# A state space mixer with its matrix products in four column groups of TensorE, and its gate placed behind two tiles of the output projection

## The chip, the cores and the metric

The kernel runs on one core of a Trainium2 chip. TensorE (PE) multiplies and writes to PSUM, VectorE (DVE), ScalarE (ACT) and GpSimd (POOL) compute, SyncE (SP) issues the DMAs. The metric is the time of one execution on the device in microseconds (us), median of the runs; lower is better.

## The reference, cut to what matters

Four network blocks work on 512 tokens of width 1024. The change touches the third, whose mixer joins a diagonal state space (256 channels in 16 groups of 16, with 64 states each) and a gated spatial unit (768 channels):

```python
def s5_mixer(u, ...):
    bb_re = z_re * br - z_im * bi
    bb_im = z_re * bi + z_im * br
    x_re = jnp.einsum('bsgh,gph->bsgp', uf, bb_re)
    x_im = jnp.einsum('bsgh,gph->bsgp', uf, bb_im)
    ...
    _, _, h_re, h_im = lax.associative_scan(combine, (a_re, a_im, x_re, x_im), axis=1)
    y = (jnp.einsum('bsgp,ghp->bsgh', h_re, c_re)
         - jnp.einsum('bsgp,ghp->bsgh', h_im, c_im))
    y = (y + d_skip.reshape(SSM_GROUPS, SSM_GROUP) * uf).reshape(bsz, s, SSM_WIDTH)
    y = jax.nn.gelu(y)
    y = y * jax.nn.sigmoid(y @ w_glu + b_glu)
...
        mix = jnp.concatenate([a_out, b_out], axis=-1) @ ev_w_out[e]
    h = h + mix
    h = h + conv_ffn(rmsnorm(h, ffn_norm_g[layer]), ...)
```

## The kernel before

All activations lie transposed, 128 channels by 512 tokens in a tile. A product of accuracy close to float32 is made of three matmuls of split operands (`mm3`, L533, whose lines L535, L536 and L537 appear in the trace): each operand is cut by `split` (L496: a cast on ACT, a subtraction on DVE) or, for weights, by `wsplit` (L510: cast L518, subtraction L519 on DVE or POOL) into a high and a low part. One `mm3` piece, as the text calls it, is one such matmul. Products of whole float32 operands show as two records each.

The order of instructions on each engine is set when the program is built: a list scheduler with a model of the engines goes through the code in priority order and fixes one order per engine. On the chip each engine then takes its instructions strictly in that order, and waits where an operand isn't there.

The stage is `ev` (L1233). It makes the 256 state space inputs `u32` (L1267, after the norms of `ev_norms`, L1212), the value half of the gated unit (192 pieces of 384 columns, in two halves), then for six heads the gate half (144 pieces of 512 columns) and `spatial` (L1294). Between them the generator `s5` (L1468) is stepped by `next(s5)`. It treats the 1024 states as eight indices `i` of 128 states; per index:

- `prepare` (L1479) forms the input matrix from B and z (ACT L1486, DVE L1487), transposes it on PE (L1491) and splits it (L1494, L1495); `inputs` (L1497) puts 32 channels three times into a tile `us` (L1502 to L1504); two matmuls (L1533) follow.
- The rotation by the tables `cs` and `sn`: four products on DVE out of PSUM (L1538, L1539, L1541, L1542), a sum and a difference on POOL (L1540, L1543).
- Two scans on DVE (L1547, L1548), and the rotation back: two products on DVE (L1550, L1552), two on POOL (L1551, L1553), one difference each on DVE (L1554, `hr`) and POOL (L1555, `hi`).
- Two float32 matmuls of 128 rows (L1522, L1523) add the result to the tile `py`, four indices to each.

When a half of 128 channels is complete: L1526, a gelu (L1527), a split. After all eight indices come the matmuls of `w_glu`, the sigmoid and the gate (L1331, L1332). The output projection takes 18 pieces per tile `f` from the gated unit (`ew_oa`) and 6 from the state space (`ew_ob`, in `rest`, L1343), 204 pieces with the 12 of `w_glu`; `resid` (L594) adds each tile to `x` and prepares the next stage (`ffn`). `scaled` (L1341) multiplies the eight tiles of `x` by the norm before they are added to.

## Time and profile before

| | |
|---|---|
| median of 3 runs | 1980.95 us (1980.42 to 1981.53) |
| the profiled execution | 1977.64 us, its span 1975.6 us, granted clock 0.984 |
| busy in the span | PE 96%, weight loads 81%, DVE 64%, ACT 47%, POOL 30% |
| the chain that ended last | PE 46%, DVE 4%, ACT 1%, issue 1% of the span in pieces that it lists by name |

The busy share of PE is that of the whole span; for the stage of the change it stands in the rows below. Of every group of instructions the rows give the number, the time that it was busy and the mean duration of one; instructions of one engine overlap by a little, so the step from one start to the next is shorter than the duration.

### The profile page before, as it was taken

The page shows a single profiled execution, that of the slowest core. Times are in us where ns is not written, and L with a number is a line of the kernel's source. Part 1 is how long each engine was busy: PE and PEld are TensorE (multiplying, and loading weights), DVE is VectorE, ACT ScalarE, POOL GpSimd, SP SyncE. Part 2 cuts the span into 40 slices and gives each one's busy share as a digit, 9 for nine tenths or more (in the row PEclk, how much of TensorE's full clock was granted, in tenths as well). Part 3 has the DMA queues.
Part 4 walks back from the last instruction along what each step waited for, and adds up shares of the span by engine and source line. Part 5 has one row for each costly group of instructions (what it writes and reads, how often), then busy time and mean ns, then how long its engine had stood idle before and what let it go on. Part 6 is the DMA issues. An engine that isn't in the chain of part 4 may idle for free.

```text
span 1975.6 us, 25804 instructions
## 1 busy us (share of the span) xinstructions
PE 1887.0 (96%) x10098; PEld 1599.0 (81%) x10098; DVE 1272.2 (64%) x1801; ACT 932.0 (47%) x1601; POOL 591.6 (30%) x514
## 2 busy tenths in 40 slices
PE   7999999999989999897889999999999999999997
PEld 4788889898879899786668888888788888888886
DVE  4422777777565555889976666666744566666666
ACT  4534677677365544756535333333422343333333
POOL 0012766654012221656630313131400002121213
PEclk8999999999999999999999999999999999999998
DMA  8531000103321111132113232223222222222221
GB/s 332 192 123 59 28 17 12 44 23 109 106 77 62 43 43 49 65 107 91 48 56 126 86 107 85 107 86 107 85 86 91 101 88 104 91 102 89 103 88 62
DMA packets 31833, 171.81 MB, mean 87 GB/s; under 512 B 3328, under 2 KB 6656, under 8 KB 14688
## 3 DMA queue, kind: packets, MB, share of 16 engines
q1 hardware_dynamic: 31712, 170.17, 24.1%
q8 instruction: 79, 1.29, 0.3%
q14 instruction: 42, 0.34, 0.1%
HBM read 168.06 MB, written 2.10 MB: 86 GB/s over the span
## 4 chain that ended last, share of the span: by engine, by line
PE 46%; DVE 4%; issue 1%; ACT 1%; POOL 0%; DVEq 0%; POOLq 0%; ACTq 0%
PE b L535 15%; PE b L537 15%; PE b L536 15%; DVE cv L1564 0%; DVE x L1683 0%; DVE hl L502 0%; DVE wl L519 0%; DVE hr L1554 0%; DVE x L598 0%; ACT wh L518 0%; PE b L624 0%; DVE yl L498 0%; DVE gt L1301 0%; POOL cv L1595 0%; DVE b L1547 0%
## 5 line engine op out<-in xcount | busy, mean ns | idle before, releaser
L535 PE MATMUL b<-hh,wh 128*128 128x512 f32 (+1 forms) x1248 | 482.2, 389 | 4.0 <-DVE uu L1305 2.7
L518 ACT CAST wh<-raw 128x1024 fp32r<-128x1024 f32 (+1 forms) x257 | 263.4, 1026 | 463.5 <-PE b L536 418.7
L536 PE MATMUL b<-hl,wh 128*128 128x512 f32 (+1 forms) x1248 | 477.6, 383 | 3.7 <-DVE hl L502 3.7
L537 PE MATMUL b<-hh,wl 128*128 128x512 f32 (+1 forms) x1248 | 477.6, 383 | 0.0
L519 DVE TENSOR_TENSOR wl<-raw,wh 128x1024 fp32r<-128x1024 f32 (+1 forms) x189 | 239.9, 1272 | 86.1 <-ACT wh L518 76.7
L519 POOL TENSOR_TENSOR wl<-raw,wh 128x1024 fp32r<-128x1024 f32 (+1 forms) x68 | 166.2, 2446 | 418.6 <-ACT wh L518 418.4
L535 PEld LDWEIGHTS b<-hh,wh 128*128 128x128 f32 x1248 | 235.3, 189 | 56.7 <-issue 7.7
L536 PEld LDWEIGHTS b<-hl,wh 128*128 128x128 f32 x1248 | 235.9, 189 | 53.6 <-DVE hl L502 4.9
L537 PEld LDWEIGHTS b<-hh,wl 128*128 128x128 f32 x1248 | 235.6, 189 | 49.5 <-issue 0.4
L1564 DVE SCALAR_TENSOR_TENSOR cv<-u,vec,cv 128x511 f32<-128x511 f32 x192 | 184.1, 959 | 41.3 <-ACT cv L1562 39.3
L1590 DVE TENSOR_TENSOR u<-b,Rp 128x512 f32<-128x512 f32 x88 | 60.8, 691 | 157.9 <-PE b L537 157.6
L535 PE MATMUL b<-ah,wh 128*128 128x512 f32 (+1 forms) x368 | 140.1, 382 | 0.0
L537 PE MATMUL b<-ah,wl 128*128 128x512 f32 (+1 forms) x368 | 140.0, 381 | 0.0
L536 PE MATMUL b<-al,wh 128*128 128x512 f32 (+1 forms) x368 | 139.8, 380 | 0.0
L1595 POOL TENSOR_TENSOR cv<-cv 128x512 f32<-128x512 f32 x44 | 57.1, 1297 | 269.3 <-DVE cv L1564 212.9
L1615 DVE TENSOR_TENSOR x<-x,b 128x512 f32<-128x512 f32 x160 | 105.7, 680 | 12.4 <-PE b L537 12.1
L535 PE MATMUL b<-wh,hh 128*128 128x256 f32 (+1 forms) x320 | 96.2, 303 | 2.6 <-ACT wh L518 2.6
L1562 ACT ACTIVATE cv<-u,vec 128x512 f32<-128x512 f32 x96 | 78.2, 814 | 35.7 <-DVE u L1590 35.7
L536 PE MATMUL b<-wl,hh 128*128 128x256 f32 (+1 forms) x320 | 93.7, 294 | 0.0
L537 PE MATMUL b<-wh,hl 128*128 128x256 f32 (+1 forms) x320 | 93.0, 292 | 0.0
L1050 DVE TENSOR_REDUCE st<-b 128x1 f32<-128x768 f32 (+1 forms) x96 | 74.1, 773 | 28.4 <-PE b L537 27.8
L1055 POOL TENSOR_SCALAR p<-p,st 128x768 f32<-128x768 f32 (+1 forms) x96 | 73.2, 764 | 56.1 <-DVE st L1054 49.5
(406 smaller groups left out, 3878.6 us busy)
## 6 DMA issues: line engine op xcount, KB each, us to landing
raw<-in_fw_up SPq DMA_DIRECT2D x44, 1024.0 KB, 4.8
raw<-in_fw_dn SPq DMA_DIRECT2D x22, 1024.0 KB, 4.8
raw<-in_ow_in SPq DMA_DIRECT2D x12, 1024.0 KB, 4.8
ada<-in_ada SPq DMA_DIRECT2D x8, 1024.0 KB, 11.4
raw<-in_mw_in SPq DMA_DIRECT2D x7, 1024.0 KB, 7.9
spare<-in_ada SPq DMA_DIRECT2D x5, 1024.0 KB, 6.5
cq<-in_ada SPq DMA_DIRECT2D x4, 1024.0 KB, 5.0
raw<-in_mw_out SPq DMA_DIRECT2D x4, 1024.0 KB, 4.9
```

The lines of the kernel that those rows point to most:

```text
L518: self.S.copy(hi, raw[:, o:o + w])
L519: (leng or self.V).tensor_tensor(lo, raw[:, o:o + w], hi.bitcast(F32), op=ALU.subtract)
L535: m(out, w[0], x[0], start=start, stop=False)
L536: m(out, w[0], x[1], start=False, stop=False)
L537: m(out, w[1], x[0], start=False, stop=stop)
L1050: V.tensor_reduce(st[:, 0:1], sv, axis=AX.XY, op=ALU.max, negate=True)
L1055: G.tensor_scalar(p[:, :nk * P], p[:, :nk * P], st[:, 2:3], 0.0, op0=ALU.mult, op1=ALU.add)
L1562: self.S.activation(v, u, AF.Identity, bias=col(3), scale=col(2))
L1564: self.V.scalar_tensor_tensor(v[:, sh:], u[:, :T - sh], col(tap), v[:, sh:], op0=ALU.mult, op1=ALU.add)
L1590: V.tensor_tensor(u, ps, R, op=ALU.mult)
L1595: G.tensor_tensor(cv[0], cv[0], cv[1], op=ALU.mult)
L1615: V.tensor_tensor(self.x[:, 4 * j + f], self.x[:, 4 * j + f], ps, op=ALU.add)
```

## The change

What it does, in six parts:

1. The input matrices are plain B, laid out by the host in the order that the matmul needs (`in_s5b`, four loads of two indices each); the factor z is put into C instead (`cz`, six small DVE operations once, and a `sel` of 128x32 that adds four groups). The transposes and `bb` go; a split of B remains once for two indices.
2. `us` gets two buffers and is copied on ACT from the split halves `uh`, `ul` (three copies of 32 rows); the subtraction on DVE goes.
3. `turned` keeps the first rotation as it was, with one scratch tile `t` for both subtrahends; it runs one index ahead of `states`.
4. `states` makes the four products of the back rotation on DVE and adds nothing; `outputs` multiplies each of the four by its 128x32 matrix into its own 32 rows of one PSUM tile (four column groups), ACT copies the tile to `po`, and a matmul with `sel` adds the four groups into 32 rows of `py`. 24 of the 40 POOL operations of the eight indices go.
5. The generator is stepped after other tiles of the value and gate parts, and `uu` and `sg` have one buffer in place of two.
6. The pieces of `ew_oa` for the first two tiles (`first(0)`, `first(1)`) stand ahead of `w_glu`; `scaled` stands behind the last product of the state space (`behind`, an order without a wait).

The diff; the lines that it takes out of `s5` are those of the listing above.

```diff
...
+    b, c = np.zeros((32, 8, 2, P), w.dtype), np.zeros((P, 8, 2, 32), w.dtype)
+    for part, nm in enumerate(("re", "im")):
+        for i in range(8):
+            for j in range(2):
+                ch, st = slice(16 * j, 16 * j + 16), slice(64 * j, 64 * j + 64)
+                b[ch, i, part, st] = f[f"s5_b_{nm}_2"][0][2 * i + j].T
+                c[st, i, part, ch] = f[f"s5_c_{nm}_2"][0][2 * i + j].T
+    a["s5b"] = np.concatenate([b.reshape(32, 4, 4 * P).transpose(1, 0, 2)] * 3, 1)
+    a["s5c"] = c.reshape(P, 8 * 2 * 32)
...
             uh, ul = yh[:, 0:2], yl
+            next(s5)
             us = []
...
-            next(s5)
...
-                    next(s5, None)
+                    if kg % 2 == half:
+                        next(s5, None)
...
-                uu = M.tile([P, T], F32, tag="uu", name="uu", bufs=2)
+                uu = M.tile([P, T], F32, tag="uu", name="uu", bufs=1)
...
+            win = self.wstream(ins["ew_oa"], 8, 2, P)
+            parts = {}
+            def first(f):
+                if f < KT:
+                    w, ps = next(win), self.b1()
+                    for k in range(6):
+                        self.mm3(ps, (w[0][:, k], w[1][:, k]), (yh[:, 2 + k], yl[2 + k]), k == 0, False)
+                    parts[f] = ps
+            first(0)
+            first(1)
             w, = self.wload(ins["w_glu"], 512)
...
-            win = self.wstream(ins["ew_oa"], 8, 2, P)
 
             def scaled(f):
                 if f < KT:
-                    V.scalar_tensor_tensor(x[:, f], x[:, f], self.vcol("final_g", f), R, op0=ALU.mult, op1=ALU.mult)
-
-            def rest(f, ps):
+                    i = V.scalar_tensor_tensor(x[:, f], x[:, f], self.vcol("final_g", f), R, op0=ALU.mult, op1=ALU.mult)
+                    self.behind(i, self.s5_last)
+
+            def rest(f):
+                scaled(f)
+                ps = parts.pop(f)
                 for k in range(2):
                     c = slice(f % 4 * P, (f % 4 + 1) * P)
                     self.mm3(ps, (wb[0][:, k, c], wb[1][:, k, c]), (yh[:, k], yl[k]), False, k == 1)
                 self.resid(f, ps, self.vcol("ffn_norm_g_2", f))
 
-            scaled(0)
-            before = None
-            for f in range(KT):
-                w = next(win)
-                scaled(f + 1)
-                ps = self.b1()
-                for k in range(6):
-                    self.mm3(ps, (w[0][:, k], w[1][:, k]), (yh[:, 2 + k], yl[2 + k]), k == 0, False)
-                if f:
-                    if f % 4 == 1:
-                        wb = self.view(self.wload(ins["ew_ob"][f // 4], 1024)[0], 512)
-                    rest(f - 1, before)
-                before = ps
+            for g in range(2):
+                first(4 * g + 2)
+                if g:
+                    rest(2)
+                first(4 * g + 3)
+                if g:
+                    rest(3)
+                wb = self.view(self.wload(ins["ew_ob"][g], 1024)[0], 512)
+                rest(4 * g)
+                first(4 * g + 4)
+                rest(4 * g + 1)
+                first(4 * g + 5)
+            rest(6)
             self.look_ahead(True, "fw_up0", 2 * NFF)
-            rest(KT - 1, before)
+            rest(7)
...
+        US = {}
+        BH, RAW = {}, {}
+        def load(n):
+            if n < 4:
+                RAW[n] = Z.tile([96, 2, 2, P], F32, tag="braw", name="braw", bufs=1)
+                self.dma(RAW[n].rearrange("p i a s -> p (i a s)"), self.ins["s5b"][n])
+        def prepare(n):
+            if n < 4:
+                BH[n] = Z.tile([96, 2, 2, P], F32R, tag="bh", name="bh", bufs=2)
+                S.copy(BH[n], RAW[n])
+                V.tensor_tensor(BH[n][64:96], RAW[n][64:96], BH[n][64:96].bitcast(F32), op=ALU.subtract)
+                load(n + 1)
+        cc = Z.tile([P, 8, 2, 32], F32, tag="us", name="cc", bufs=2)
+        self.dma(cc.rearrange("p i a c -> p (i a c)"), self.ins["s5c"])
+        load(0)
+        yield
+        cz = Z.tile([P, 2, 8, 32], F32, name="cz")
+        ct = Z.tile([P, 8, 32], F32, name="ct")
+        zr, zi = (self.s5c[nm].unsqueeze(2).to_broadcast([P, 8, 32]) for nm in ("zr", "zi"))
+        re, im = cc[:, :, 0], cc[:, :, 1]
+        V.tensor_tensor(ct, im, zi, op=ALU.mult)
+        V.tensor_tensor(cz[:, 0], re, zr, op=ALU.mult)
+        V.tensor_tensor(cz[:, 0], cz[:, 0], ct, op=ALU.subtract)
+        V.tensor_tensor(ct, re, zi, op=ALU.mult)
+        V.tensor_tensor(cz[:, 1], im, zr, op=ALU.mult)
+        V.scalar_tensor_tensor(cz[:, 1], cz[:, 1], -1.0, ct, op0=ALU.mult, op1=ALU.subtract)
+        sel = Z.tile([P, 32], F32, name="sel32")
+        V.tensor_reduce(sel, self.ident.rearrange("p (j c) -> p c j", j=4), axis=AX.X, op=ALU.add)
+        prepare(0)
+        yield
         def inputs(i):
             if i >= 8:
                 return
...
+            if i % 4 == 0:
+                self.split(uh[:, i // 4], ul[i // 4], u32[:, i // 4])
+            US[i] = Z.tile([96, T], F32R, tag="us", name="us", bufs=2)
+            rows = slice(32 * (i % 4), 32 * (i % 4) + 32)
+            for j, u in enumerate((uh[rows, i // 4], ul[i // 4][rows], uh[rows, i // 4])):
+                S.copy(US[i][32 * j:32 * j + 32], u.bitcast(F32))
         def tmp(name, bufs=1):
             return self.s5_pool.tile([P, T], F32, tag=name, name=name, bufs=bufs)
...
+        def turned(i):
+            cs, sn = self.cs[:, i], self.sn[:, i]
+            pp = [self.b1(), self.b1()]
+            for part, ps in enumerate(pp):
+                PE.matmul(ps, BH[i // 2][:, i % 2, part], US[i], start=True, stop=True)
+            if i % 2 == 0:
+                prepare(i // 2 + 1)
+            inputs(i + 1)
+            out = []
+            for nm, op, (p, q) in (("a", ALU.add, pp), ("d", ALU.subtract, pp[::-1])):
+                r, t = tmp(nm, 2), tmp("t")
+                V.tensor_tensor(r, p, cs, op=ALU.mult)
+                V.tensor_tensor(t, q, sn, op=ALU.mult)
+                G.tensor_tensor(r, r, t, op=op)
+                out.append(r)
+            return out
+        def states(i, a, d):
+            cs, sn = self.cs[:, i], self.sn[:, i]
+            mg = col("mag", i).to_broadcast([P, T])
+            b, e = tmp("b"), tmp("e")
+            V.tensor_tensor_scan(a, mg, a, 0.0, op0=ALU.mult, op1=ALU.add)
+            V.tensor_tensor_scan(d, mg, d, 0.0, op0=ALU.mult, op1=ALU.add)
+            V.tensor_tensor(b, a, cs, op=ALU.mult)
+            V.tensor_tensor(a, a, sn, op=ALU.mult)
+            V.tensor_tensor(e, d, cs, op=ALU.mult)
+            self.s5_last = V.scalar_tensor_tensor(d, d, -1.0, sn, op0=ALU.mult, op1=ALU.mult)
+            return b, d, a, e
+        def outputs(i, prods):
+            ps = self.b1()
+            for g, x in enumerate(prods):
+                PE.matmul(ps[32 * g:32 * g + 32], cz[:, g // 2, i], x, start=True, stop=True)
+            po = tmp("po", 2)
+            S.copy(po, ps)
+            return po
+        inputs(0)
+        nxt = turned(0)
         yield
...
+        for i in range(8):
+            cur = nxt
+            if i < 7:
+                nxt = turned(i + 1)
+            po = outputs(i, states(i, *cur))
+            h, g = i // 4, i % 4
+            if g == 0:
+                py = self.b1()
+            if g % 2 == 0:
+                before = po
+            else:
+                for j, x in ((g - 1, before), (g, po)):
+                    PE.matmul(py[32 * j:32 * j + 32], sel, x, start=True, stop=True)
+            if g == 3:
+                V.scalar_tensor_tensor(u32[:, h], u32[:, h], self.vcol("s5_d_2", h), py, op0=ALU.mult, op1=ALU.add)
+                S.activation(u32[:, h], u32[:, h], AF.Gelu_apprx_tanh)
+                self.split(uh[:, h], ul[h], u32[:, h])
+            yield
```

On DVE, an index in the middle of the value and gate parts. Before (`hr` ends an index, `wl` is a weight split, `uu` belongs to the gated unit):

```order
L1554 TENSOR_TENSOR hr<-hr,a 128x512
L1495 TENSOR_TENSOR bh<-b_9440,bh 32x256
L1487 SCALAR_TENSOR_TENSOR bb<-bc,s5zr,bb 128x128 x2
L1538 TENSOR_TENSOR a<-b_9431,cs 128x512
L1542 TENSOR_TENSOR e<-b_9431,sn 128x512
L1541 TENSOR_TENSOR d<-b_9432,cs 128x512
L1291 TENSOR_REDUCE rs<-ss 128x4
L1305 TENSOR_TENSOR uu<-b_9535,RR 128x512
L519 TENSOR_TENSOR wl<-raw,wh 128x1024
L1547 SCALAR_TENSOR_TENSOR b<-s5mag,a 128x512
L1504 TENSOR_TENSOR us<-u_8926,us 32x512
L1548 SCALAR_TENSOR_TENSOR e<-s5mag,d 128x512
```

And with the change, from one last product of an index (L1563) to the next (the line numbers are those of the changed file; L1558 and L1559 are the scans, L1560 to L1563 the four products, L1547 and L1548 the first rotation):

```order
L1548 TENSOR_TENSOR t<-b_9529,sn 128x512
L1558 SCALAR_TENSOR_TENSOR a<-s5mag,a 128x512
L1560 TENSOR_TENSOR b<-a,cs 128x512
L515 TENSOR_TENSOR wl<-raw,wh 128x1024
L1559 SCALAR_TENSOR_TENSOR d<-s5mag,d 128x512
L1561 TENSOR_TENSOR a<-a,sn 128x512
L1547 TENSOR_TENSOR a<-b_9618,cs 128x512
L1548 TENSOR_TENSOR t<-b_9619,sn 128x512
L1547 TENSOR_TENSOR d<-b_9619,cs 128x512
L1562 TENSOR_TENSOR e<-d,cs 128x512
L1563 SCALAR_TENSOR_TENSOR d<-d,sn 128x512
```

The operations of two indices are interleaved, and the small ones on 128 or 256 elements are gone.

On PE, around the last product of the last index. Before, 42 pieces of `yh` and `w` (output projection and `w_glu`) stand ahead of it; these are the last of them:

```order
L535 MATMUL b_10054<-yh,wh 128x512
L536 MATMUL b_10054<-yl,wh 128x512
L537 MATMUL b_10054<-yh,wl 128x512
L1522 MATMUL py<-hr,bc 128x512
L1523 MATMUL py<-hi,bc 128x512
L535 MATMUL b_10096<-yh,wh 128x512
```

With the change (L531 to L533 are `mm3`, L1296 the spatial product, L1570 `outputs`, L1590 the sum by `sel`):

```order
L1296 MATMUL b_9913<-wt,vt 128x128 x4
L1296 MATMUL b_9931<-wt,vt 128x128
L1570 MATMUL b_9867<-d,cz 32x512
L1570 MATMUL b_9867<-a,cz 32x512
L1570 MATMUL b_9867<-e,cz 32x512
L1296 MATMUL b_9931<-wt,vt 128x128 x3
L531 MATMUL b_9953<-yh,wh 128x512
...
L531 MATMUL b_9976<-yh,wh 128x512
L1590 MATMUL b_9651<-po,sel_8947 32x512
L532 MATMUL b_9976<-yl,wh 128x512
```

None of the 204 pieces stands ahead of the last products now; 19 stand between them and the last sum, 185 behind it. Earlier on PE, 68 pieces of the value part stand between the norms and the first L1540 (the input product), where 86 stood ahead of the first L1533 before.

## Rows read from the trace of the kernel before

**Rows 1.** Busy time by stretch: start to end, length, then engines, granted clock, DMA.

```profile
876.04:1011.84 135.80, 110.09 (x489) 88.06 (x488) 129.25 (x150) 67.50 (x174) 79.67 (x49) 0.94 0.18 61
891.76:1010.66 118.90, 93.25 (x397) 72.14 (x395) 116.18 (x130) 59.57 (x160) 73.98 (x48) 0.93 0.17 59
```

**Rows 2.** Who waited for whom, 891.7 to 1011.9 us: total, times, longest.

```profile
PE py L1522 <- DVE hr L1554: 8.7, 3, 4.5
...
PE b L1533 <- DVE bh L1495: 5.7, 3, 2.5
...
DVE a L1538 <- PE b L1533: 2.7, 1, 2.7
DVE hr L1554 <- POOL a L1551: 1.4, 1, 1.4
```

**Rows 3.** DVE in order of time, beginning of the stage: start, duration, instruction.

```profile
876.17 0.35 DVE L1487 SCALAR_TENSOR_TENSOR bb<-bc,s5zr,bb 128x128 f32<-128x128 f32 x1
...
877.16 5.39 DVE L1341 SCALAR_TENSOR_TENSOR x<-x,vec,evR 128x512 f32<-128x512 f32 x8
...
891.76 0.69 DVE L1538 TENSOR_TENSOR a<-b,cs 128x512 f32<-128x512 f32 x1 [2.74 <-PE b L1533]
```

**Rows 4.** DVE in order of time, stretches in which nothing holds it up.

```profile
963.97 1.21 DVE L519 TENSOR_TENSOR wl<-raw,wh 128x1024 fp32r<-128x1024 f32 x1
...
983.72 0.67 DVE L1538 TENSOR_TENSOR a<-b,cs 128x512 f32<-128x512 f32 x1
984.32 0.67 DVE L1542 TENSOR_TENSOR e<-b,sn 128x512 f32<-128x512 f32 x1
...
988.11 0.42 DVE L1495 TENSOR_TENSOR bh<-b,bh 32x256 fp32r<-32x256 f32 x1
...
989.68 1.21 DVE L1547 TENSOR_TENSOR_SCAN b<-s5mag,a 128x512 f32<-128x512 f32 x1
990.82 1.20 DVE L1548 TENSOR_TENSOR_SCAN e<-s5mag,d 128x512 f32<-128x512 f32 x1
```

**Rows 5.** DVE by group, 891.7 to 1010.7 us: count, busy us, mean ns, idle before.

```profile
L1550 DVE TENSOR_TENSOR hr<-b,cs 128x512 f32<-128x512 f32 x8 | 10.2, 1269 | 0.1
...
L1538 DVE TENSOR_TENSOR a<-b,cs 128x512 f32<-128x512 f32 x8 | 5.5, 684 | 2.8 <-PE b L1533 2.7
```

**Rows 6.** By group: POOL from 1060 to 1975 us, then PE from 876.1 to 1051.6.

```profile
L1595 POOL TENSOR_TENSOR cv<-cv 128x512 f32<-128x512 f32 x44 | 57.1, 1297 | 269.3 <-DVE cv L1564 212.9 <-issue 56.5
...
L1299 PE MATMUL b<-wt,vt 128*128 128x128 f32 x48 | 6.6, 276 | 1.4 <-DVE gt L1301 1.4
```

**Rows 7.** PE in order of time, in the value part.

```profile
876.04 0.42 PE L535 MATMUL b<-wh,hh 128*128 128x384 f32 x1
...
891.33 0.63 PE L1533 MATMUL b<-us,bh 96*128 96x512 f32 x2
...
908.13 1.02 PE L1522 MATMUL py<-hr,bc 128*128 128x512 f32 x2
908.99 1.02 PE L1523 MATMUL py<-hi,bc 128*128 128x512 f32 x2
```

**Rows 8.** PE in order of time, an earlier stage with 32 and 64 columns.

```profile
567.65 0.39 PE L257 MATMUL b<-hl,wr 128*32 128x512 f32 x1
567.89 0.39 PE L259 MATMUL b<-hh,wr 128*64 128x512 f32 x1
568.11 0.39 PE L536 MATMUL b<-hl,wh 128*128 128x512 f32 x1
```

**Rows 9.** DVE, then PE in order of time, end of the stage.

```profile
1008.92 1.73 DVE L1554 TENSOR_TENSOR hr<-hr,a 128x512 f32<-128x512 f32 x1 [1.37 <-POOL a L1551]
...
1011.84 1.98 PE L1523 MATMUL py<-hi,bc 128*128 128x512 f32 x2
...
1051.39 0.40 PE L535 MATMUL b<-hh,wh 128*128 128x512 f32 x1
...
1056.67 0.39 PE L537 MATMUL b<-hh,wl 128*128 128x512 f32 x1
```

More of the change, by code (lines that the diff above doesn't have):

```diff
@@ L142, in layout @@
     a["ws_t"] = np.ascontiguousarray(f["gm_w_s_2"][0].transpose(2, 0, 1).reshape(P, 6 * P))
-    parts = []
-    for nm in ("b", "c"):
-        for part in ("re", "im"):
-            v = f[f"s5_{nm}_{part}_2"][0]
-            v = v if nm == "b" else v.transpose(0, 2, 1)
-            out = np.zeros((P, 8, P), v.dtype)
-            for i in range(8):
-                for j in range(2):
-                    for c in (0, 32, 64) if nm == "b" else (32 * (i % 4),):
-                        col = c + 16 * j
-                        out[64 * j:64 * j + 64, i, col:col + 16] = v[2 * i + j]
-            parts.append(out)
-    a["s5bc"] = np.stack(parts, 2).transpose(1, 0, 2, 3).reshape(8, P, 4 * P)
+    b, c = np.zeros((32, 8, 2, P), w.dtype), np.zeros((P, 8, 2, 32), w.dtype)
[7 more added lines that the diff above has]
+    a["s5c"] = c.reshape(P, 8 * 2 * 32)
     a["w_glu"] = _units(f["s5_w_glu_2"][0], 2, 256)[0]
@@ L1329, in ev @@
             for f, ps in enumerate(pg):
-                sg = M.tile([P, T], F32, tag="uu", name="sg", bufs=2)
+                sg = M.tile([P, T], F32, tag="uu", name="sg", bufs=1)
                 S.activation(sg, ps, AF.Sigmoid, bias=self.vcol("s5_b_glu_2", f))
@@ L1471, in s5 @@
         col = lambda nm, i: self.s5c[nm][:, i:i + 1]
-        BC, BH, US = {}, {}, {}
-        def load(i):
-            if i < 8:
-                BC[i] = Z.tile([P, 4, P], F32, tag="bc", name="bc", bufs=4)
-                self.dma(BC[i].rearrange("p a b -> p (a b)"), self.ins["s5bc"][i])
-        def prepare(i):
-            if i >= 8:
-                return
-            re, im = BC[i][:, 0], BC[i][:, 1]
-            bb = Z.tile([P, 2, P], F32, tag="bb", name="bb", bufs=1)
-            for part, (p, q) in enumerate(((re, im), (im, re))):
-                S.activation(bb[:, part], q, AF.Copy, scale=col("zi", i))
-                V.scalar_tensor_tensor(bb[:, part], p, col("zr", i), bb[:, part], op0=ALU.mult,
-                                       op1=ALU.add if part else ALU.subtract)
-            ps = self.b1()[:, :256].rearrange("p (a b) -> p a b", a=2)
-            for part in range(2):
-                PE.transpose(ps[:, part], bb[:, part], self.ident)
-            BH[i] = Z.tile([96, 2, P], F32R, tag="bh", name="bh", bufs=2)
-            S.copy(BH[i], ps[:96])
-            V.tensor_tensor(BH[i][64:96], ps[64:96], BH[i][64:96].bitcast(F32), op=ALU.subtract)
+        US = {}
@@ L1499, in inputs @@
                 return
-            u = u32[32 * (i % 4):32 * (i % 4) + 32, i // 4]
-            US[i] = Z.tile([96, T], F32R, tag="us", name="us", bufs=1)
-            S.copy(US[i][0:32], u)
-            S.copy(US[i][64:96], u)
-            V.tensor_tensor(US[i][32:64], u, US[i][0:32].bitcast(F32), op=ALU.subtract)
+            if i % 4 == 0:
+                self.split(uh[:, i // 4], ul[i // 4], u32[:, i // 4])
+            US[i] = Z.tile([96, T], F32R, tag="us", name="us", bufs=2)
+            rows = slice(32 * (i % 4), 32 * (i % 4) + 32)
```

48 lines of the change are left out of this document (removed).

## The prediction

> **What bounds the kernel now.** I read the views in this order: busy time by stretch, the waits of PE and DVE, then the two engines in order of time. Over the whole span PE is busy 96%, so a gain must come from a stretch in which it is not. The page's slices show one, between 875 and 1012 us, and there busy time by stretch tells who is full: from 876.04 to 1011.84 us DVE is busy 129.25 of 135.80 us and PE 110.09, so PE stands idle for 25.7 us, at a granted clock of 0.94 [rows 1]. The waits name the cause: PE waits for `hr`, the last DVE product of an index, and for `bh`, the split of the input matrix, while DVE waits for PE only at the start (2.7 us) and for POOL once (1.4) [rows 2]. So DVE is the bound from the first rotation product at 891.76 [rows 3] to the end of the last `hr` at 1008.92 + 1.73, about 1010.66 [rows 9], 118.9 us. PE then has dense work until the next stage starts at 1051.39 [rows 9].
>
> DVE's 118.9 us are not all work. Two-operand instructions of 512 elements follow each other by 0.60 us where nothing disturbs them, scans by 1.13 [rows 4]. A product that reads PSUM (L1538) takes 684 ns on the mean, the same product out of SBUF alone (L1550) 1269 [rows 5]. POOL is busy 73.98 us of the stretch, with 48 instructions [rows 1], and what it reads lies in SBUF. The slow ones on DVE are those whose two operands both lie there too.
>
> **The change, part by part.** Every sum is made in the profiled execution (1977.64 us), which lies 3.3 below the median of 1980.95; a difference is carried over to the median unchanged.
>
> *DVE's own work, first rotation product to last product.* In the order before there are 84 instructions of 512 elements (50.4 us at 0.60), 16 scans (18.1), six weight splits of 1024 elements (6.8, as long as a scan, 1.21 against 1.21 [rows 4]), three of 768 (2.6), seven `bh` at 0.42 [rows 4] (2.9), twelve `bb` (3.7 at 0.31, just under the 0.35 of one [rows 3]): 84.6 us. In the new order, 80 of 512 elements (48.0), the same 16 scans and nine splits: 75.6. The state space itself is lighter by 4.7 (two products more and one difference less per index; `us`, `bb` and most `bh` gone); the other 4.3 us (seven instructions of the gated unit) only stand later, behind the last product.
>
> *What POOL takes from DVE.* 118.9 - 84.6 leaves 34.3 us above clean work, for 48 POOL instructions 0.71 us each. The new order has 21 in that stretch (16 sums, three of the gated unit, two weight splits): 15.0 us. I charge it per instruction, since the excess sits on instructions that read SBUF only [rows 5].
>
> *Start.* 18 pieces fewer stand ahead of the first input product. 86 pieces took 876.04 to 891.33 [rows 7], 0.178 each, so the first rotation product comes 3.2 us earlier, at 888.6. The inputs are there: the eight `scaled` (5.39 us [rows 3]), which stood between the norm and `u32`, go behind the last product. There they cost nothing, since DVE next waits for the last sum on PE anyway; without that cover, 5.4 us. DVE's pace alone thus ends at 888.6 + 75.6 + 15.0 = 979.2.
>
> *PE's own work, from 876.04 to the last products.* 192 pieces of 384 columns (34.2 us), 144 of 512 at 0.2296 (24 took 1051.39 to 1056.67 [rows 9]; 33.1), spatial products (6.6 us for all [rows 6]; 21 of 24, 5.8), 16 input products at a piece each (3.7), seven sums by `sel` and the four group products of eight indices. A whole float32 product is two records and steps by 0.86 (908.13 to 908.99 [rows 7]): the sums are 6.0 us. No row shows products in different column groups. If the later three of an index overlap fully, an index takes 1.72 us (the first of them stands apart); if nothing overlaps, 3.43. I take 2.57: the second record of a product needs the group of the first, so only the neighbours' records can lie side by side. Eight indices: 20.6 us, ends 13.7 and 27.5. PE's pace alone ends at 979.4 (972.5 to 986.3).
>
> A rule speaks against the groups. An earlier stage goes from 32 columns to 64 to 128, and the starts stay 0.22 to 0.24 apart [rows 8]: no emptying of the array. The Trainium skill, TensorEngine Tiling (Array Packing), Key Properties, says that changing the tiling mode drains TensorE. By the rows the 38 changes of width in the new order cost nothing; by that rule, each would cost up to what a record outlasts its step. I take the rows, and the rule goes to the first rival.
>
> *Mutual waits.* Both paces now end at 979, so neither engine has slack to run ahead. The first product tile `e` and the scratch `t` have one buffer, and `uu` has one now: DVE stands in line for PE and POOL, with scans and splits behind it. At least what DVE waited after its start before, 1.4 us; at most PE's idle time less the waits for `bh`, whose split is now prepared a pair ahead: 25.7 - 5.7 = 20.0 [rows 1, 2]. I take the middle, 10.7, since PE gives up as much slack as DVE gains. Last product: 979.4 + 10.7 = 990.1.
>
> *Tail.* Three products (1.72), six spatial records (0.8), all 204 pieces (46.8), one sum (0.86), and 1.0 for the half clock after a wait (the last L1523 took 1.98 behind a wait [rows 9], 1.02 elsewhere [rows 7]): 51.2 us. Before it was 40.7, because 42 pieces had filled earlier gaps. So 10.5 us are given back here. The gate's chain (sum, gelu, split, sigmoid) is covered by the pieces of the first four tiles.
>
> *The rest.* ACT gets copies of 32 rows and `po`, and loses `bb` and its share of `bh`; it is busy 59.57 of 118.90 us [rows 1], so nothing. Five loads replace eight on SP's queue at a DMA share of 0.17 [rows 1]: nothing; late, they would hold the first split.
>
> Sum: next stage at 990.1 + 51.2 = 1041.3 in place of 1051.39, 10 us less. Median **1971.0 us**. With the ends of the waits: 1032.0 (1961.6 us) and 1050.6 (1980.2).
>
> **The rivals.**
> 1. *PE becomes the bound, slower.* The groups run one after another and each change of width empties the array: 986.3, and 38 times 0.16 (a record of 0.39 less a step of 0.23 [rows 8]) makes 992.4, the tail 52.4. It decides from 6.6 us of waits on, as 992.4 + 6.6 + 52.4 is 1051.4. With all 20.0: 1064.8, 1994 us. For it: PE is strictly in order and each index waits for two sets of products. Against: rows 8 show no emptying.
> 2. *POOL holds DVE for whole instructions.* An undisturbed POOL sum takes 1.297 us [rows 6]. If each of the 21 costs DVE all of it, 27.2 in place of 15.0: DVE's pace 991.4, with waits 1002.1, next stage 1053.3, 1983 us. The rows have 0.71 on the mean, but the sums now stand close to DVE instructions on SBUF. The Trainium skill, SBUF — State Buffer, Who interferes with whom, states that a DVE instruction with two SBUF inputs and a GpSimd instruction that reads SBUF block each other for a whole instruction; by that rule this price is the ceiling, and the trace agrees that only the SBUF products are slowed [rows 5].
> 3. *No mutual waits.* The scheduler's order fits: 1962 us or a little less.
>
> **How the numbers follow.** A measurement of this kernel can tell about 0.2%, 4 us, from no change. Forecast 0.72 (0.05 of it within 4 us); rival 3, 0.06; rival 2, 0.12 (0.02 faster, 0.08 same, 0.02 slower); rival 1, 0.10 (0.02 same, 0.08 slower). Faster 0.75, same 0.15, slower 0.10. The range runs between the ends of the waits, 1961 to 1980; rival 1 and half of rival 2 lie outside.
>
> **What would show it.** Right: between 876 and 1000 us PE idle falls to about 11 to 20 us, POOL to some 30 us of busy time, products out of SBUF near 0.8 to 0.9 us; the last state space product near 990; then 185 pieces without a gap. Column groups: starts of the second and third product under 0.86 us apart. Wrong: starts 0.86 apart with gaps around them (rival 1); SBUF products still at 1.27 us (rival 2); a wait of PE for `yl` behind the last sum would break the tail.

## The result and the profile after

The changed kernel takes **1969.27 us** (median of 4 runs, 1969.06 to 1971.18) where the kernel before, timed beside it, takes 1980.68 (1979.38 to 1981.53): a ratio of 0.9945, with a 95% interval of 0.9928 to 0.9962. That is faster by about 11 us, between 7.5 and 14 by the interval; 10 were forecast. The profiled execution took 1969.1 us, its span 1967.4.

Busy time by stretch, the changed kernel (columns as in [rows 1]); the stretches are from the start of the stage to the last product of the state space, from the first rotation product to that, and from there to the next stage:

```profile
876.25:987.52 111.27, 99.70 (x451) 69.74 (x450) 101.24 (x120) 69.75 (x171) 39.28 (x23) 0.97 0.20 68
891.58:987.52 95.94, 85.08 (x371) 55.62 (x369) 92.48 (x108) 58.10 (x150) 37.43 (x22) 0.96 0.18 63
987.52:1041.33 53.81, 52.78 (x237) 41.63 (x236) 33.28 (x45) 23.21 (x34) 2.59 (x2) 1.00 0.26 95
```

POOL fell from 48 instructions and 73.98 us [rows 1] to 22 and 37.43; DVE's stretch from 118.90 to 95.94 us, and DVE is still busy 96% of it. PE's idle time up to the last product is 111.27 - 99.70 = 11.6 us, where it was 25.7. The next stage starts at 1041.33 in place of 1051.39 [rows 9].

The same comparison over the whole stage, up to the next one, before and after:

```profile
876.04:1051.39 175.35, 149.64 (x652) 119.76 (x652) 154.85 (x183) 86.42 (x202) 79.67 (x49) 0.94 0.20 71
```

```profile
876.25:1041.33 165.08, 152.49 (x687) 111.37 (x686) 134.53 (x164) 92.96 (x204) 41.86 (x25) 0.98 0.22 77
```

On PE, which is what the next stage waits for, 10.3 us went: its idle time fell by 13.1 (25.71 to 12.59), its busy time rose by 2.9. The new order has some 7 us more work on PE, an estimate from its rows: eight sums of 0.86, 38 changes of width at about 0.1 (see below), less some 3 us of transposes that are gone; the group products take about as long as the 16 products that they replace. That the rise is smaller goes with the granted clock, 0.98 in place of 0.94: after waits PE runs at the lower of its two levels, 1.2 GHz in place of 2.4, for a while, and there are fewer waits now. The first product `b`, behind a wait of 4.20 us, took 1.92 us for its two records, the next one 1.04.

Who waited for whom on DVE and PE, the stage after the change:

```profile
DVE wl L515 <- ACT wh L514: 6.7, 4, 2.6
PE b L1570 <- DVE b L1560: 6.2, 2, 4.2
...
PE b L1296 <- ACT vt L1293: 2.1, 1, 2.1
...
PE b L1570 <- DVE d L1563: 1.8, 2, 0.9
...
DVE e L1562 <- PE b L1570: 1.6, 1, 1.6
```

The waits for `bh` and for `hr` [rows 2] are gone. So is one that stood between these two in the view of the kernel before, and that the prediction doesn't name:

```profile
PE b L535 <- DVE uu L1305: 7.1, 2, 4.3
```

Of PE's 25.7 us of idle time before, 8.7 were for `hr`, 7.1 for the gated unit's `uu` and 5.7 for `bh`. Of the 12.6 now, 8.0 are for the products `b` and `d`. The wait for `uu` doesn't come back in the experiments below that undo the POOL part or the generator's steps, so what removed it stays open. PE now stands once for 4.2 us in front of the first product `b` of the first index. DVE by group, 888 to 990 us (columns as in [rows 5]):

```profile
L1559 DVE TENSOR_TENSOR_SCAN d<-s5mag,d 128x512 f32<-128x512 f32 x8 | 12.3, 1542 | 0.0
...
L1558 DVE TENSOR_TENSOR_SCAN a<-s5mag,a 128x512 f32<-128x512 f32 x8 | 10.7, 1337 | 0.0
L1560 DVE TENSOR_TENSOR b<-a,cs 128x512 f32<-128x512 f32 x8 | 8.0, 998 | 0.3
...
L1561 DVE TENSOR_TENSOR a<-a,sn 128x512 f32<-128x512 f32 x8 | 6.4, 798 | 0.0
L1547 DVE TENSOR_TENSOR a<-b,cs 128x512 f32<-128x512 f32 x8 | 5.5, 682 | 1.1 <-PE b L1540 0.9
```

Products out of SBUF take 0.80 to 1.00 us now, where one took 1.27 [rows 5]; those out of PSUM keep their 0.68. PE in order of time, the other three products of the first index:

```profile
910.56 0.34 PE L532 MATMUL b<-wl,hh 128*128 128x384 f32 x1
910.83 0.62 PE L1570 MATMUL b<-d,cz 128*32 128x512 f32 x1
910.84 0.62 PE L1570 MATMUL b<-a,cz 128*32 128x512 f32 x1
910.84 0.62 PE L1570 MATMUL b<-e,cz 128*32 128x512 f32 x1
911.28 0.59 PE L1570 MATMUL b<-d,cz 128*32 128x512 f32 x1
911.29 0.59 PE L1570 MATMUL b<-a,cz 128*32 128x512 f32 x1
911.30 0.59 PE L1570 MATMUL b<-e,cz 128*32 128x512 f32 x1
911.82 0.44 PE L533 MATMUL b<-wh,hl 128*128 128x384 f32 x1
```

Column groups work: three products start within 0.01 us of each other and together take as long as one. The row before them steps by 0.27 us in place of 0.17, and the last record by 0.52, where its group stepped by 0.45: each change of width costs some 0.1 us. On the way in it is the width and not the type that costs: before, the step into a float32 product of 128 columns was the usual 0.17 (907.96 to 908.13).

### The profile page after: what moved, and what is told of

It reads as the page before. It is cut to its first block, busy times and chain, and to the rows that moved or that the text cites. A ratio compares the mean times of both kernels' runs of the same rounds, so it can differ in the third digit from the quotient of the medians.

```text
span 1967.4 us, 25809 instructions
## 1 busy us (share of the span) xinstructions
PE 1889.8 (96%) x10130; PEld 1589.5 (81%) x10130; DVE 1258.6 (64%) x1790; ACT 938.0 (48%) x1599; POOL 553.5 (28%) x490
## 4 chain that ended last, share of the span: by engine, by line
PE 79%; DVE 11%; ACT 5%; issue 2%; DMA 2%; POOL 1%; SPq 0%; DVEq 0%; POOLq 0%; ACTq 0%
PE b L531 23%; PE b L533 23%; PE b L532 23%; PE b L1060 2%; PE b L378 1%; PE b L1071 1%; PE b L1072 1%; DVE wl L515 1%; PE b L736 1%; DMA ada<-in_ada 1%; DVE hl L498 1%; DVE ql L494 1%; ACT wh L514 1%; DVE f L1470 1%; DVE st L1046 1%
## 5 line engine op out<-in xcount | busy, mean ns | idle before, releaser
L531 PE MATMUL b<-hh,wh 128*128 128x512 f32 (+1 forms) x1248 | 481.1, 389 | 0.2 <-ACT hh L682 0.2
L533 PE MATMUL b<-hh,wl 128*128 128x512 f32 (+1 forms) x1248 | 478.2, 384 | 0.0
L515 DVE TENSOR_TENSOR wl<-raw,wh 128x1024 fp32r<-128x1024 f32 (+2 forms) x189 | 235.1, 1247 | 83.3 <-ACT wh L514 70.4
L531 PEld LDWEIGHTS b<-hh,wh 128*128 128x128 f32 x1248 | 234.9, 189 | 57.1 <-issue 11.0
L533 PEld LDWEIGHTS b<-hh,wl 128*128 128x128 f32 x1248 | 235.4, 189 | 50.3 <-issue 1.3
L531 PE MATMUL b<-ah,wh 128*128 128x512 f32 (+1 forms) x368 | 140.1, 382 | 0.0
L533 PE MATMUL b<-ah,wl 128*128 128x512 f32 (+1 forms) x368 | 140.0, 381 | 0.0
L1653 DVE TENSOR_TENSOR x<-x,b 128x512 f32<-128x512 f32 x160 | 105.6, 681 | 11.6 <-PE b L533 11.3
L531 PE MATMUL b<-wh,hh 128*128 128x256 f32 (+1 forms) x320 | 96.4, 303 | 2.6 <-ACT wh L514 2.6
L533 PE MATMUL b<-wh,hl 128*128 128x256 f32 (+1 forms) x320 | 93.4, 293 | 0.0
```

The source lines that it names most:

```text
L515: (leng or self.V).tensor_tensor(lo, raw[:, o:o + w], hi.bitcast(F32), op=ALU.subtract)
L531: m(out, w[0], x[0], start=start, stop=False)
L533: m(out, w[1], x[0], start=False, stop=stop)
L1653: V.tensor_tensor(self.x[:, 4 * j + f], self.x[:, 4 * j + f], ps, op=ALU.add)
```

## The experiments

Each is the changed kernel with one edit, so a diff is against that. Times are medians; ratios are to the kernel before, timed beside it, with 95% intervals.

**The changed kernel again.** 

> The changed kernel again, as the measure for the others: 1967 to 1971 us.

Measured 1969.74 us, 0.9954 (0.9942 to 0.9966). The next stage starts at 1041.34, PE's idle time over the whole stage is 11.6 us (12.6 above): the gain repeats, 9 us by the ratio, and 0.9954 is what the others are held against.

**No column groups.**

```diff
...
-                PE.matmul(ps[32 * g:32 * g + 32], cz[:, g // 2, i], x, start=True, stop=True)
-            po = tmp("po", 2)
-            S.copy(po, ps)
...
+                PE.matmul(py[32 * j:32 * j + 32], cz[:, g // 2, i], x, start=(g == 0), stop=(g == 3))
...
-                for j, x in ((g - 1, before), (g, po)):
-                    PE.matmul(py[32 * j:32 * j + 32], sel, x, start=True, stop=True)
...
```

> The four products of an index go one after another into the same 32 rows of py; the sums by sel and the copies po are gone. On PE an index then costs 3.43 us in place of about 1.8 (13 us more for eight), and the seven sums of 0.86 fall away: 7 us more of PE work. Theory (DVE bounds the stretch up to the last product, PE has some 11 us of idle time there): the idle time takes most of it, 1968 to 1972 us. Rival (PE bounds the stretch): all 7 us come through, 1976 us.

Measured 1969.46 us, 0.9959 (0.9947 to 0.9971). In the trace the three products after `b` start 0.89 and 0.85 us apart, so they do run one after another. By the medians it makes no difference; the profiled execution, with a span of 1973.7, was the slowest of its runs, and there the next stage starts 5.5 us later, at 1046.81; 3.0 of these are a late start of the rotation (893.83 against 890.83), whose cause stands below under *Start*. As the theory has it, the gain doesn't hang on products side by side.

**The back rotation's sums on POOL again.**

```diff
             V.tensor_tensor(b, a, cs, op=ALU.mult)
+            G.tensor_tensor(e, d, sn, op=ALU.mult)
             V.tensor_tensor(a, a, sn, op=ALU.mult)
-            V.tensor_tensor(e, d, cs, op=ALU.mult)
-            self.s5_last = V.scalar_tensor_tensor(d, d, -1.0, sn, op0=ALU.mult, op1=ALU.mult)
-            return b, d, a, e
+            G.tensor_tensor(d, d, cs, op=ALU.mult)
+            self.s5_last = V.tensor_tensor(b, b, e, op=ALU.subtract)
+            G.tensor_tensor(a, a, d, op=ALU.add)
+            return b, a
...
```

Two products per index are left for PE, in two column groups.

> The back rotation as in the kernel before: two products and both sums per index, three of the six operations on POOL; two column groups in place of four. DVE does 8 instructions fewer (4.8 us less), POOL 24 more. Theory (a POOL instruction takes 0.8 us from DVE): 24 x 0.8 - 4.8 = 14 us more on DVE, which bounds, 1979 to 1984 us. Rival (POOL holds DVE for its whole instruction, 1.3 us): 26 us more, 1990 to 1996. Rival (POOL takes nothing from DVE, PE bounds): 1964 to 1970.

Measured 1993.02 us, 1.0069 (1.0056 to 1.0082): more than the whole gain is lost. The number lies in the range of the rival that charges whole POOL instructions, but the trace speaks against its mechanism. Busy time from the first rotation product to the last product, the repeated changed kernel first, then this one:

```profile
890.83:987.54 96.71, 86.09 (x373) 56.54 (x371) 92.49 (x108) 58.23 (x150) 37.46 (x22) 0.95 0.19 62
```

```profile
893.49:1007.91 114.42, 82.24 (x324) 53.73 (x322) 94.25 (x99) 57.16 (x148) 75.92 (x45) 0.85 0.16 52
```

DVE's busy time rose by 1.8 us with 9 instructions fewer (5.4 at 0.60), so 23 POOL instructions took 7.2 us, 0.3 each, not 0.8 and not 1.3. Its idle time rose by 16 (4.2 to 20.2), of which only 2.4 us were spent waiting for POOL itself. (The start of this execution is 2.7 us later for the reason under *Start* below.) The waits of this version, 876.25 to 1041 us:

```profile
PE b L1572 <- DVE b L1564: 26.7, 4, 12.6
...
DVE wl L515 <- ACT wh L514: 13.9, 6, 6.3
...
ACT wh L514 <- PE b L533: 6.8, 2, 3.4
...
DVE a L1547 <- PE b L1540: 5.7, 1, 5.7
```

Read together, these waits make a ring: PE stands in front of a product that DVE hasn't made; meanwhile it frees no weight tile, so ACT can't cast the next (`wh`), and DVE, in order, stands at the split of that weight, or at the rotation for which PE hasn't made the input yet.

**All four products at once.**

```diff
-            for g, x in enumerate(prods):
-                PE.matmul(ps[32 * g:32 * g + 32], cz[:, g // 2, i], x, start=True, stop=True)
+            last = PE.matmul(ps[32:64], cz[:, 0, i], prods[1], start=True, stop=True)
+            for g in (0, 2, 3):
+                m = PE.matmul(ps[32 * g:32 * g + 32], cz[:, g // 2, i], prods[g], start=True, stop=True)
+                self.behind(m, last)
```

> The first of the four products of an index is held back on PE until the last one is ready, so that all four overlap: PE does 8 x 0.86 = 6.9 us less. Theory (DVE bounds): PE waits as much longer, 1966 to 1971 us. Rival (PE bounds): 1962 us.

Measured 1987.49 us, 1.0043 (1.0031 to 1.0055): less work on PE, and 18 us slower than the changed kernel. Neither theory had this. The scheduler put all four where `b` alone had stood, 24 pieces behind the input products of the second index. PE, then DVE, in order of time:

```profile
905.44 1.06 PE L1569 MATMUL b<-d,cz 128*32 128x512 f32 x1 [11.81 <-DVE d L1563]
905.45 1.06 PE L1571 MATMUL b<-b,cz 128*32 128x512 f32 x1
905.46 1.06 PE L1571 MATMUL b<-a,cz 128*32 128x512 f32 x1
905.46 1.06 PE L1571 MATMUL b<-e,cz 128*32 128x512 f32 x1
906.30 1.06 PE L1569 MATMUL b<-d,cz 128*32 128x512 f32 x1
```

```profile
909.23 0.68 DVE L1563 SCALAR_TENSOR_TENSOR d<-d,sn 128x512 f32<-128x512 f32 x1
916.93 0.69 DVE L1547 TENSOR_TENSOR a<-b,cs 128x512 f32<-128x512 f32 x1 [7.02 <-PE b L1540]
```

Four products do start within 0.02 us. But PE stood 11.81 us for the last of them; then it ran at the lower clock (0.86 from a record to the next of its group, in place of 0.45) and had 48 pieces ahead of the input products for which DVE, after 909.9, had to wait 7.02 us. Over its whole stretch DVE's busy time is less than in the changed kernel (88.85 against 92.49 us), its idle time 18.7 in place of 4.2. The engines wait in turn.

**The first rotation's sums on DVE.**

```diff
-                G.tensor_tensor(r, r, t, op=op)
+                V.tensor_tensor(r, r, t, op=op)
```

> The 16 sums of the first rotation go from POOL to DVE. Theory (a POOL instruction takes some 0.8 us from DVE, a DVE instruction 0.60): DVE gains 16 x 0.8 = 12.8 us and pays 9.6, and no scan waits for a slow POOL sum any more: 3 to 6 us faster than the changed kernel, 1963 to 1967 us. Rival (the sums on POOL cost DVE nothing): 9.6 us more on DVE, which bounds, 1975 to 1980 us.

Measured 1970.15 us, 0.9962 (0.9950 to 0.9975): no difference to the changed kernel, and so in neither range. DVE by group, 888 to 990 us:

```profile
L1558 DVE TENSOR_TENSOR_SCAN a<-s5mag,a 128x512 f32<-128x512 f32 x8 | 9.7, 1216 | 0.0
L1559 DVE TENSOR_TENSOR_SCAN d<-s5mag,d 128x512 f32<-128x512 f32 x8 | 9.7, 1214 | 0.0
...
L1560 DVE TENSOR_TENSOR b<-a,cs 128x512 f32<-128x512 f32 x8 | 5.9, 736 | 0.0
...
L1561 DVE TENSOR_TENSOR a<-a,sn 128x512 f32<-128x512 f32 x8 | 5.4, 670 | 0.0
```

With 16 POOL instructions gone, the scans fall from 1542 and 1337 ns to 1214 and 1216, the products from 998 and 798 to 736 and 670: what was slow was slow because of POOL. DVE's busy time in its stretch is 90.23 us in place of 92.49 with 16 sums more (9.6 us), so a sum on POOL had cost it (9.6 + 2.3) / 16 = 0.74 us, hardly more than doing it itself.

**The gate ahead of the projection, as before.**

```diff
-            first(0)
-            first(1)
             w, = self.wload(ins["w_glu"], 512)
...
             self.open_stat()
+            first(0)
+            first(1)
```

> The matmuls of w_glu stand again ahead of the first two tiles of the output projection in the code. Theory (the chain from the last sum over gelu, split and sigmoid is covered by the other pieces in either order): 1967 to 1971 us, no difference. Rival (the gate's chain is bared): PE waits some 5 us for it, 1973 to 1976 us.

Measured 1970.42 us, 0.9960 (0.9947 to 0.9974). No difference: other pieces cover the gate's chain in either order.

**`scaled` early.**

```diff
-                    i = V.scalar_tensor_tensor(x[:, f], x[:, f], self.vcol("final_g", f), R, op0=ALU.mult, op1=ALU.mult)
-                    self.behind(i, self.s5_last)
+                    V.scalar_tensor_tensor(x[:, f], x[:, f], self.vcol("final_g", f), R, op0=ALU.mult, op1=ALU.mult)
```

> The eight products scaled are no longer held behind the last product of the state space, so they stand early, ahead of u32. Theory (DVE bounds from its first rotation product on, and this comes later by up to the 5.4 us of these eight, less what DVE waits there for a weight cast, 2.6): 1970 to 1974 us. Rival (DVE had time there): 1967 to 1970 us.

Measured 1973.68 us, 0.9976 (0.9967 to 0.9985): 4 us slower than the changed kernel, as the theory has it. The norm's result `RR` ends at 889.56 (883.48 with the change), the first rotation product comes at 895.17 (891.58): 3.6 us later (4.2 with the earlier load of this execution allowed for, see *Start* below): the wait of 2.6 us for the weight cast is covered now, one of 2.2 for the input product stands in its place. PE waits 10.1 us for the first `b` in place of 4.2.

**The copies `us` by DMA.**

```diff
-                S.copy(US[i][32 * j:32 * j + 32], u.bitcast(F32))
+                if i:
+                    self.nc.scalar.dma_start(out=US[i][32 * j:32 * j + 32].bitcast(F32), in_=u.bitcast(F32))
+                else:
+                    S.copy(US[i][32 * j:32 * j + 32], u.bitcast(F32))
```

> The copies us of the indices 1 to 7 are made by DMAs that ACT issues, in place of 21 ACT copies of 0.62 us. Theory (ACT is no bound, but three of these copies stand ahead of the weight cast for which DVE waits 2.6 us before the first rotation): 0 to 2 us faster, 1965 to 1969 us. Rival (a copy by DMA lands later and PE waits for it, or ACT's queue is held by the issue): 1971 to 1978 us.

Measured 1965.54 us, 0.9939 (0.9926 to 0.9951), some 3 us faster than the changed kernel by the ratios, though the intervals overlap. DVE at the beginning, the changed kernel first, then this one:

```profile
890.70 0.96 DVE L515 TENSOR_TENSOR wl<-raw,wh 128x768 fp32r<-128x768 f32 x1 [2.63 <-ACT wh L514]
891.58 0.69 DVE L1547 TENSOR_TENSOR a<-b,cs 128x512 f32<-128x512 f32 x1
```

```profile
887.34 0.96 DVE L515 TENSOR_TENSOR wl<-raw,wh 128x768 fp32r<-128x768 f32 x1 [0.75 <-ACT wh L514]
888.22 0.68 DVE L1550 TENSOR_TENSOR a<-b,cs 128x512 f32<-128x512 f32 x1
```

The weight cast `wh` had stood on ACT behind the six copies of the first two indices; with three of them gone DVE waits 1.9 us less for it. (The other 1.5 us of the difference lie ahead of the copies: `RR` ends at 882.01 in place of 883.48. That part differs between executions of every version, see *Start* below.)

**Copies by DMA and sums on DVE.** Both edits. 

> Copies us by DMA and the 16 sums on DVE together. Theory (a sum costs DVE the same 0.6 to 0.8 us on either engine, the copies' gain stays): as with the copies by DMA alone, 1964 to 1968 us. Rival (with ACT free and no POOL sum to wait for, DVE runs without gaps): 1959 to 1963 us.

Measured 1962.86 us, 0.9917 (0.9901 to 0.9932): the fastest so far, some 7 us faster than the repeated changed kernel, its interval clear of that one's. The median lies below the theory's range and in the rival's. Against the copies alone the intervals overlap, and the two profiled executions have the same span, 1963.3 us, and the same start of the next stage, 1037.4. But here the first rotation product came 2.7 us later (890.90 against 888.22, see *Start* below), and the stretch from it to the last product was 2.4 us shorter (93.01 against 95.36). So the traces speak for a gain of 2 to 3 us by the sums beside the copies; the medians neither show nor exclude it.

**POOL idle.** Also the gated unit's products (`gt`) and the four weight splits of POOL on DVE. 

> As the version with the copies by DMA and the sums on DVE, and the six products of the gated unit and the four weight splits of the value part go to DVE as well, so POOL has nothing left beside DVE in the stage. Theory (such an instruction costs DVE about the same on either engine): no difference to that version, 1960 to 1966 us. Rival (the last POOL instructions still hold DVE for longer than it would need itself): 1955 to 1960 us. Rival (they were free on POOL): 1966 to 1972 us.

Measured 1962.86 us, 0.9924 (0.9911 to 0.9938): no difference to the version before it, with no POOL instruction from the first rotation product to the last product. Products out of SBUF take 0.67 to 0.69 us there, as those out of PSUM do, and the scans 1.22: with POOL idle nothing is left of what slowed DVE. Against the copies alone DVE has 22 POOL instructions less beside it and 23 instructions more of its own, and its busy time falls by 2.8 us (93.51 to 90.73).

**All four products at once, but later.** With the copies by DMA; the outputs of an index are written after the next rotation, and the last product gets `self.behind(last, self.lastmm)`, where `lastmm` is the latest `mm3` piece of the program so far. 

> The four products of an index together, as before in one experiment, but placed behind all pieces that the program has up to the next index (the first set 72 pieces later in place of 24), with the copies us by DMA. Theory (what made the four together slow was PE standing 31 us in front of them, not the products): that wait falls under 10 us, 1960 to 1969 us. Rival (four products at once cost more than three and one, or DVE now waits for PE to free the product tiles): 1975 to 1990 us.

Measured 1972.80 us, 0.9962 (0.9948 to 0.9976): 15 us better than the quadruple in its first place, of which the copies are worth some 4; so the place was most of its loss. But PE still waits 18.6 us for `d`, more than the 10 expected, and the version is slower than the same without this edit (1965.54, timed apart, the intervals just overlapping): it lies above the theory's range and below the rival's.

**The generator's steps as before.**

```diff
-                    if kg % 2 == half:
-                        next(s5, None)
+                    next(s5, None)
```

> The generator is stepped after each of the eight groups of the value part, as in the kernel before, in place of four. The first products then stand 27 pieces behind the first input product in both versions, but the second and third index come earlier on PE. Theory (PE, strictly in order, meets products that DVE has not made yet, stands, frees no weight tiles, and DVE waits for the casts): PE waits for products rise from some 8 us to over 15, 1975 to 1990 us. Rival (the order of steps does not matter while DVE bounds): 1967 to 1971 us.

Measured 1982.59 us, 1.0014 (1.0005 to 1.0022): with the steps of before the whole gain is gone. The last product comes 15 us *earlier*, at 972.28, and the next stage 12 us later, at 1053.80. Busy time from the first rotation product to the last product, and PE's waits for products, 876.25 to 1041 us:

```profile
890.43:972.28 81.85, 62.04 (x237) 34.15 (x236) 81.03 (x93) 50.07 (x138) 33.72 (x18) 0.77 0.15 51
```

```profile
PE b L1569 <- DVE d L1562: 13.6, 4, 7.5
...
PE b L1569 <- DVE b L1559: 5.3, 2, 2.7
```

DVE is full (81.03 of 81.85 us), with fewer instructions of other kinds between those of the state space. PE stands in front of the products for 18.9 us (8.0 with the change), at a granted clock of 0.77, and has 81.5 us of work left behind the last product, where it had 53.8. Over the whole stage its idle time is 20.5 us (12.6 with the change) and its busy time 157.1 (152.5) at a granted clock of 0.89 (0.98): of the 12.5 us by which the next stage is later, some 8 are waits and some 5 the same work taking longer. The waits rose as the theory said; its second half, that DVE then waits for casts, isn't seen here.

## Why the prediction was right, by its steps

*The bound.* DVE from the first rotation product to the last product: right. Serial products, with more work on PE, take the same median; a start of DVE that comes 3.6 us later (`scaled` early) costs 4 us, and an earlier one (copies by DMA) gains. But PE's order has to fit, or DVE no longer bounds: with the old steps DVE made its last product 15 us earlier, and the next stage came 12 us later (part 5, below). The reading of the waits left out the second longest, 7.1 us for `uu`.

*What POOL takes from DVE.* Mis-sized a little. Forecast 21 x 0.71 = 15.0; the stretch took 95.94 us less 3.5 idle, less 75.6 clean: 16.9 for 22, 0.77 each, and 0.74 by the experiment. The clean work was counted right (80 instructions of 512 elements, 16 scans, nine splits). The 0.71 was read too high, since the 118.9 us that it starts from hold 2.7 us in which DVE stood idle (116.18 busy, [rows 1]); without them it is 0.66. POOL's own busy time is 37.4 us, where some 30 were expected. That a POOL instruction holds DVE for a whole instruction (rival 2) isn't borne out as a price: 1.3 each would be 28.5. But it isn't a constant either: with 45 POOL instructions it was 0.3, where DVE stood idle for 20.2 of 114.4 us; why it was lower there wasn't tried.

*Start.* Forecast 888.6, measured 891.58: the step that failed most. The pieces ahead of the input product did fall as counted, but this product began only at 889.22, 0.71 us late for its copies `us`, and DVE had a weight split ahead of the rotation, whose cast stood on ACT behind six copies `us`. Two terms had been put at nothing, and both were wrong.

The first is the loads ("nothing; late, they would hold the first split"). The tile `braw` has one buffer, so the second pair of input matrices is loaded only when the split of the first is made (issued at 874.81, as that split ends). ACT, in fixed order, stood for it, with the norm behind:

```profile
877.10 0.62 ACT L1497 CAST bh<-braw 96x512 fp32r<-96x512 f32 x1 [6.01 <-DMA braw<-in_s5b]
...
878.36 0.68 ACT L559 ACTIVATE evq<-b,eps 128x512 f32<-128x512 f32 x1
```

On this norm hang `RR`, the inputs and their copies. In the eight profiled executions that have the copies on ACT and `scaled` late, this cast started anywhere between 874.50 and 879.35, and the first rotation product followed 14.48 to 14.50 us later every time. At 874.50 (four products at once) the rotation came at 888.98, close to the forecast. So the load explains most of the 3.0 us, and it also spreads the profiled executions by some us whatever the edit.

The second is the copies ("ACT gets copies ... so nothing"): an engine that is half idle can still be late at one place. In the three versions with the copies by DMA and the products in their places, the distance from the same cast is 12.58 to 12.59 us: the 1.9 us of the experiment.

*PE's own work.* Mis-sized twice, in opposite directions. The groups were taken as 2.57 us per index; they take about 0.9 for `b` and 0.9 for the other three (two records of 0.45), 1.8 in all, near the lower end: some 6 us less for eight. "Only the neighbours' records can lie side by side" was right, but it takes away nothing: the first records of three products run together, then their second ones. The changes of width were costed at nothing by [rows 8]; they cost some 0.1 us each, by estimate 3 to 4 us for 38. The Trainium skill, TensorEngine Tiling (Array Packing), Key Properties, says that changing the tiling mode drains TensorE. The trace agrees for changes between 128 and 32 columns, at some 0.1 us in place of the 0.16 that I had given to rival 1; the earlier stage of [rows 8] shows no such cost.

*Mutual waits.* 10.7 us were charged on top of DVE's pace of 979.2; the last product came at 987.52, 8.3 above it: 3.0 from the late start, 1.9 from POOL, 3.5 from DVE's idle time. So the waits were a third of what was charged, and two other terms filled their place. That the next stage came at 1041.33, where 1041.3 was forecast, is partly luck: the errors of the start (+3.0), of POOL (+1.9), of the waits (-7.2) and of PE's lag behind DVE (+2.9, next step) cancel. What was right is the mechanism, DVE's stretch getting shorter and PE's idle time with it, and the size of the tail.

*Tail.* Forecast 51.2, measured 53.81. PE was 2.9 us behind DVE: it made the last three products at 990.46. From there to 1041.33 it took 50.9. The late gap of the forecast was there with another cause: not the half clock, but 1.02 us for a weight cast at 1005.53.

*Part 5.* The prediction gave the generator's steps no price of their own. Undoing them costs 12 to 13 us, more than the change gains. The forecast held because the order read from the program spread the products well, not because any order would do: with four products at once, the same DVE work took 18 us longer. The rival on the slow side had its price from work on PE; what is slow in the runs is PE standing in front of products that aren't made.

What stays open is how the gain splits between POOL's part and the spread of the steps: undoing either loses all of it, so they aren't a sum. The column groups and the place of the gate, which the title names, are not needed for it by their experiments; `scaled` is worth some 4 us. Parts 1 to 3 weren't undone, and the clock's own share wasn't tried apart.

## What to carry to other kernels

Where engines run in fixed order, look first at where PE stands in front of a product that isn't made: it can hold the weight tiles too, so casts and splits on the other engines stop, and the wait comes back to the engine that was late. Fewer instructions on POOL beside a full DVE give back DVE's time (0.7 us each here, of which 0.6 are spent again if DVE does the work itself), and only if the order keeps PE off such places does the whole kernel gain; and less work on an engine that isn't the bound, such as four products in the time of one, can cost more than it saves. Before calling an engine idle enough, look at what stands in its queue ahead of the one cast that the bound engine needs, and whether a load into a single buffer stands there too.

## What the runs showed of the hardware that was not expected

Float32 products of 32 columns in different column groups start within 0.01 to 0.02 us, and three or four take the time of one (two records of 0.45 us). Going from 128 columns to 32, or back, cost about 0.1 us each time in this stage. What a POOL instruction takes from DVE varied from 0.3 to 0.77 us each; the low price stood where DVE itself was waiting for much of the time. With no POOL instruction beside it, every product of the two rotations takes 0.67 to 0.69 us on DVE, out of SBUF as out of PSUM.
